# Attention scores in two fp32r passes, decay sums from two parts of g, later constants on GpSimd, and another planned order, in a one-core hybrid decoder layer

## The chip, the cores and the metric

The kernel runs on one core of a Trainium2 chip. The metric is the device time of one execution in microseconds (us).

## What is computed

One decoder layer on x of 256 tokens by 1024 channels, in float32: a normalisation, one combined input projection (1024 to 4104 columns), a softmax attention of 8 heads (64 wide, one key block of 256, so plainly causal, with ALiBi slopes), a gated delta rule of 4 heads (128 wide, chunks of 64), an output projection and a second normalisation, added to x. What the change touches, shortened:

```python
logit_own = einsum('hqd,hkd->hqk', qc, k_own) * scale - slopes[:, None, None] * dist_own
logit_own = where(dist_own >= 0, logit_own, NEG_INF)
p = softmax(logit_own, axis=-1)
...
gc = cumsum(g, axis=-1)
decay = exp(where(causal, gc[..., :, None] - gc[..., None, :], -inf))
a = where(strict, einsum('nbhid,nbhjd->nbhij', k_beta, k) * decay, 0.0)
t_inv = triangular_solve(a + eye, eye, lower=True, unit_diagonal=True)
...
r = xf * rsqrt(mean(xf * xf, axis=-1) + RMS_EPS)
```

## The kernel before

All calls are first recorded in a `Plan` and then put in order by a list scheduler (`Plan.run`, `Plan.order`), which has its own costs for every operation. It takes among the ready operations of an engine the one with the best rank, shifted by tables at lines 376 to 391: `MARGIN` (extra slack that the plan allows for results of TensorE, of the other engines and of loads), `BATCH` (a bonus for a matmul of the same row shape as the last), and `LEAD` (a bonus or malus for each stage). `emit` (line 354) then issues them, so in the profile nearly every instruction has line L372, and tiles tell them apart.

**Precision.** A float32 product is made from two parts of 12 bits (hi and lo, type fp32r) in three passes: hi by hi, hi by lo, lo by hi. ScalarE (ACT) copies the hi part, VectorE (DVE) subtracts it to get lo. TensorE (PE) runs fp32r products, and a few plain float32 ones.

**Stages.** The weights come in groups of 512 columns: dz (z and the b and a columns of the delta rule, in 8 pieces `raw_dz`), dk, dq, dv, then av, aq, ak, az for the attention, then the output weights. Each piece is loaded by SyncE's (SP) queue, split into hi and lo tiles (`dk_hi`, `dk_lo` and so on, five buffers of each), and multiplied with the transposed, normalised x (`hhi`, `hlo`). Forty-eight small matmuls on a zero tile (`ps_warm`) are put in by the plan where the engine would otherwise be thinly used.

**Head (lines 561 to 594).** For each of two halves t of the tokens: ACT squares one half of x, DVE the other, DVE adds the two sums and the epsilon (`rx<-ssq`), GpSimd (POOL) raises to the power -0.5 (`rx<-rx,pow`), ACT and DVE each scale half of x, PE transposes it (`hT`).

**GpSimd's constants (lines 470 to 540).** `blk`, `blks`, `lvl` (masks of the block inverse), `bias0` (printed as `bias`; causal mask and distances), `qscale`, and zeros in `yz` and in `qz` are written on POOL among the head's powers.

**Decay (lines 713 to 729).** `gneg` is minus log decay. For each t DVE makes `gs` (128x512, triu times gneg), and PE sums it with the strict lower triangle `strl` into `ps_d` in plain float32, then adds a mask in bf16. ACT takes its exponential (`dT`), which goes into the matrix whose inverse is built by stages `inv` and `dbl`: the recursion over `wc`, the spread to `wT`, two 32-square transposes (`xX`), products `ps_y` and `ps_w`, a second pair of transposes, products again. The state recurrence (`rec`) follows, then the output projection.

**Scores (lines 975 to 1016).** For each of 8 heads two parts, 128x128 and 128x256, each of three passes. Heads lie in pairs in 128 rows, 64 each; `qz` holds the scaled q with zeros in the other head's 64 rows, hi and lo apart; `ka_h` and `ka_l` hold the hi and lo parts of k for two pairs at a time.

**End (lines 1102 to 1126).** Each t has stores of 512 or 256 columns, all on SP's queue.

Of the kernel before, what the change touches and what calls it, by code (L numbers as in the profile page):

```python
# [123 lines left out]
class Plan:  # L124
# [24 lines left out]
    def record(self, eng, real, name, args, kw):  # L149
# [27 lines left out]
        if after:  # L177
            op.preds[self.ops[-1]] = True
# [202 lines left out]
BATCH = 0  # L381

MARGIN = [411, 175, 0]
# [6 lines left out]
LEAD = {"out0": 3258, "dk": 2097, "inv": -3594, "av": 2525, "dbl": -402, "out1": -1204, "att0": -470, "mixd": -508, "az": -1375}  # L390
# [4 lines left out]
def tile_hybrid(  # L395
# [22 lines left out]
    def const(shape, name, dtype=F32):  # L418
        return plan.tile(sb, shape, dtype, name)
# [4 lines left out]
    def sl(tag, shape, name, dtype=F32):  # L424
        return plan.tile(sb, shape, dtype, name, tag=tag)
# [57 lines left out]
    for t in range(NT):  # L483
        G.memset(yz16[:, of_chunk[t], :], 0.0)
# [4 lines left out]
    blk = const([P, NB, BASE], "blk")  # L489
    G.memset(blk, 1.0)  # L490
    G.affine_select(out=blk, in_=blk, pattern=[[-BASE, NB], [0, BASE]], compare_op=OP.is_ge,
                    fill=0.0, base=0, channel_multiplier=1)
    G.affine_select(out=blk, in_=blk, pattern=[[BASE, NB], [0, BASE]], compare_op=OP.is_ge,
                    fill=0.0, base=BASE - 1, channel_multiplier=-1)

    blks = const([P, NB, BASE], "blks")
    G.affine_select(out=blks, in_=blk, pattern=[[BASE, NB], [1, BASE]], compare_op=OP.is_gt,
                    fill=0.0, base=0, channel_multiplier=-1)

    strl = const([P, P], "strl")  # L500
# [5 lines left out]
    V.tensor_scalar(far16, strl, -NEG, None, op0=OP.mult)  # L506
# [3 lines left out]

    nl = P // (2 * BASE)
    lvl = const([P, nl, 2, BASE], "lvl")
    G.memset(lvl[:, :, 0, :], 0.0)
    G.memset(lvl[:, :, 1, :], 1.0)
    G.affine_select(out=lvl[:, :, 1, :], in_=lvl[:, :, 1, :], pattern=[[-2 * BASE, nl], [0, BASE]],
                    compare_op=OP.is_ge, fill=0.0, base=0, channel_multiplier=1)
    G.affine_select(out=lvl[:, :, 1, :], in_=lvl[:, :, 1, :], pattern=[[2 * BASE, nl], [0, BASE]],
                    compare_op=OP.is_ge, fill=0.0, base=BASE - 1, channel_multiplier=-1)


    bias0 = const([P, P + T], "bias0")
    G.iota(bias0[:, :P], pattern=[[1, P]], base=0, channel_multiplier=-1,
           allow_small_or_imprecise_dtypes=True)
    G.affine_select(out=bias0[:, :P], in_=bias0[:, :P], pattern=[[-1, P]], compare_op=OP.is_ge,
                    fill=NEG, base=0, channel_multiplier=1)
    G.iota(bias0[:, P:], pattern=[[1, T]], base=-P, channel_multiplier=-1,
           allow_small_or_imprecise_dtypes=True)
    G.affine_select(out=bias0[:, P:], in_=bias0[:, P:], pattern=[[-1, T]], compare_op=OP.is_ge,
                    fill=NEG, base=P, channel_multiplier=1)
    slopes = [2.0 ** -(h + 1) for h in range(HA)]  # L530

    qscale = const([P, HA // 2], "qscale")
    for h in range(HA):
        b = DA * (h % 2)
        G.memset(qscale[b : b + DA, h // 2 : h // 2 + 1], (DA ** -0.5) / slopes[h])

# [133 lines left out]

    vh = const([P, NT, HA * DA], "vh", F32R)
# [43 lines left out]
    gsa = sl("ms", HBB, "gs")  # L715
# [275 lines left out]
    for half in range(2):  # L991
        plan.stage = f"att{half}"
        ps = qps[half]
        for c in range(2):
            m = 2 * half + c
            for e in range(2):
                b = slice(DA * e, DA * e + DA)
                qs_ = qscale[b, m : m + 1]
                qh, ql = qz[m][b, 0, e, :], qz[m][b, 1, e, :]
                A.activation(qh, ps[b, c, :], AF.Copy, scale=qs_)  # L1000
                V.scalar_tensor_tensor(ql, ps[b, c, :], qs_, qh, op0=OP.mult, op1=OP.subtract)
        ps = kps[half]
        hm = slice(2 * half, 2 * half + 2)
        A.activation(kh[:, hm, :], ps, AF.Copy)
        V.tensor_tensor(kl[:, hm, :], ps, kh[:, hm, :], OP.subtract)
        for pr2 in range(2):
            m = 2 * half + pr2
            pTs = []
            for e in range(2):
                h = 2 * m + e  # L1010
                qh, ql = qz[m][:, 0, e, :], qz[m][:, 1, e, :]
# [96 lines left out]
    for t in range(NT):  # L1108
# [14 lines left out]
        for c0, cn in groups[t]:  # L1123
# [32 lines left out]
```

## Time and profile before

| | |
|---|---|
| runs (median of 3) | 174.79 us (174.78 to 174.94) |
| the profiled execution, its own time | 174.88 us |
| its span | 172.9 us |
| granted clock over the span | 0.989 |
| busy share | PE 95%, PEld 89%, DVE 78%, ACT 63%, POOL 12% |

The profiled execution is 0.09 us over the median, and 1.98 us of its time lie outside the span. Busy times are sums over instructions of the durations shown; matmuls overlap in the pipeline, so a matmul's own duration is longer than the distance from its start to the next one's start, and the distance is what it costs. The granted clock stands at 1.00 in every stretch of 10 us but the last.

### The profile page before, as it was taken

How to read it: one execution, taken by the hardware profiler on the slowest of the kernel's cores; microseconds unless marked ns; L12 is line 12 of the kernel's file. 1: busy time of each engine (PE TensorE's matmuls, PEld its weight loads, DVE VectorE, ACT ScalarE, POOL GpSimd, SP SyncE). 2: the span in 40 equal slices, each digit the busy share in tenths (PEclk: the TensorE clock that was granted, in tenths of full speed). 3: DMA queues.
4: the chain of work that ended last, by engine and by line, in shares of the span. 5: the costliest groups of instructions: out<-in, count | busy, mean ns of one | idle time of the engine just before them, and what ended most of it. 6: DMA issues, size and time to landing. Idle time of an engine off the chain costs nothing.

```text
span 172.9 us, 3465 instructions
## 1 busy us (share of the span) xinstructions
PE 164.1 (95%) x1311; PEld 154.1 (89%) x1311; DVE 134.7 (78%) x330; ACT 108.8 (63%) x231; POOL 21.2 (12%) x58
## 2 busy tenths in 40 slices
PE   7799999999999999999999999999999999999950
PEld 5589999997999999989999999999999998888850
DVE  4589566799579999898798999999689676474542
ACT  3689949968785545478554575665849594671230
POOL 8950000000000300400020000000001810000110
PEclk9999999999999999999999999999999999999995
DMA  5667689995776351067676108600000000640033
GB/s 193 232 224 261 224 271 241 391 317 136 207 233 161 91 189 57 5 205 276 222 245 200 69 0 251 238 0 0 8 0 4 2 0 0 196 172 0 3 118 121
DMA packets 12326, 24.92 MB, mean 144 GB/s; under 512 B 741, under 2 KB 1046, under 8 KB 12310
## 3 DMA queue, kind: packets, MB, share of 16 engines
q1 hardware_dynamic: 12310, 24.71, 44.1%
q8 instruction: 10, 0.16, 0.4%
q14 instruction: 6, 0.05, 0.1%
HBM read 23.65 MB, written 1.05 MB: 143 GB/s over the span
## 4 chain that ended last, share of the span: by engine, by line
PE 87%; POOL 5%; issue 4%; ACT 1%; DVE 1%; POOLq 0%; DVEq 0%
PE ps_out L372 10%; PE ps_av L372 9%; PE ps_az L372 7%; PE ps_dz L372 7%; PE ps_ak L372 7%; PE ps_dq L372 7%; PE ps_aq L372 7%; PE ps_dv L372 7%; PE ps_dk L372 7%; PE ps_s L372 3%; PE ps_y L372 2%; PE ps_w L372 2%; PE ps_gb L372 2%; PE ps_pt L372 2%; PE ps_d L372 1%
## 5 line engine op out<-in xcount | busy, mean ns | idle before, releaser
L372 DVE TENSOR_TENSOR o_lo<-raw_o,o_hi 128x1024 fp32r<-128x1024 f32 x8 | 9.8, 1220 | 5.1 <-ACT o_hi L372 5.1
L372 ACT ACTIVATE o_hi<-raw_o 128x1024 fp32r<-128x1024 f32 x8 | 8.4, 1056 | 5.0 <-PE ps_az L372 2.7
L372 ACT ACT_TABLE_LOAD x8 | 10.3, 1283 | 0.9 <-PEq L1143 0.8
L372 ACT ACTIVATE att_y<-att_y,mx 128x128 f32<-128x128 f32 (+1 forms) x16 | 7.2, 448 | 4.4 <-DVE mx L372 4.4
L372 PE MATMUL ps_az<-hlo,az_hi 128*128 128x256 f32 x32 | 9.8, 305 | 0.0
L372 PE MATMUL ps_az<-hhi,az_lo 128*128 128x256 f32 x32 | 9.6, 300 | 0.0
L372 PE MATMUL ps_aq<-hlo,aq_hi 128*128 128x256 f32 x32 | 9.6, 299 | 0.0
L372 PE MATMUL ps_az<-hhi,az_hi 128*128 128x256 f32 x32 | 9.5, 297 | 0.0
L372 PE MATMUL ps_warm<-wz 128*128 128x256 bf16 x48 | 8.3, 333 | 1.1 <-DVE wz L372 1.1
L372 PE MATMUL ps_aq<-hhi,aq_hi 128*128 128x256 f32 x32 | 9.3, 291 | 0.0
L372 PE MATMUL ps_aq<-hhi,aq_lo 128*128 128x256 f32 x32 | 9.2, 291 | 0.0
L372 PE MATMUL ps_dq<-hlo,dq_hi 128*128 128x256 f32 x32 | 9.1, 286 | 0.0
L372 PE MATMUL ps_dq<-hhi,dq_lo 128*128 128x256 f32 x32 | 9.1, 289 | 0.0
L372 PE MATMUL ps_ak<-hhi,ak_lo 128*128 128x256 f32 x32 | 9.1, 284 | 0.0
L372 PE MATMUL ps_ak<-hhi,ak_hi 128*128 128x256 f32 x32 | 9.1, 284 | 0.0
L372 PE MATMUL ps_dv<-hlo,dv_hi 128*128 128x256 f32 x32 | 9.1, 283 | 0.0
L372 PE MATMUL ps_dq<-hhi,dq_hi 128*128 128x256 f32 x32 | 9.0, 283 | 0.0
L372 PE MATMUL ps_dk<-hhi,dk_hi 128*128 128x256 f32 x32 | 9.0, 286 | 0.0
L372 PE MATMUL ps_dv<-hhi,dv_lo 128*128 128x256 f32 x32 | 9.0, 280 | 0.0
L372 PE MATMUL ps_ak<-hlo,ak_hi 128*128 128x256 f32 x32 | 9.0, 280 | 0.0
L372 PE MATMUL ps_dv<-hhi,dv_hi 128*128 128x256 f32 x32 | 9.0, 280 | 0.0
L372 PE MATMUL ps_dk<-hlo,dk_hi 128*128 128x256 f32 x32 | 8.9, 280 | 0.0
(254 smaller groups left out, 635.6 us busy)
## 6 DMA issues: line engine op xcount, KB each, us to landing
raw_o<-in_w_out_dram SPq DMA_DIRECT2D x4, 1024.0 KB, 5.0
raw_dz<-in_w_in_dram SPq DMA_DIRECT2D x8, 260.0 KB, 8.1
raw_dk<-in_w_in_dram SPq DMA_DIRECT2D x2, 1024.0 KB, 9.3
raw_dq<-in_w_in_dram SPq DMA_DIRECT2D x2, 1024.0 KB, 12.9
raw_dv<-in_w_in_dram SPq DMA_DIRECT2D x2, 1024.0 KB, 9.4
raw_av<-in_w_in_dram SPq DMA_DIRECT2D x2, 1024.0 KB
raw_aq<-in_w_in_dram SPq DMA_DIRECT2D x2, 1024.0 KB, 5.9
raw_ak<-in_w_in_dram SPq DMA_DIRECT2D x2, 1024.0 KB, 7.1
```

What stands on the lines that cost most here:

```text
L372: op.call(*args, **kw)
```

## The change

1. **Scores.** q of one head is put in the head's own 64 rows as the hi part and in the other 64 rows as the lo part; the hi part of k stands in both halves; the lo part of k stands in the head's own rows, with zeros in the other. One pass then gives hi by hi plus lo by hi, a second hi by lo. k is therefore split by (head, pair) in pieces of 64x256: 16 copies on ACT, 8 subtractions on DVE. The zeros are in `kl` instead of `qz`.
2. **Decay.** gneg is itself split (`gh`, `gl`), `gs` is made for both parts, and `strl` is fp32r, so that each t has two fp32r passes instead of one plain float32 product. The two parts lie in the slots `ms` and `wT`.
3. **GpSimd.** `blk`, `blks`, `lvl`, `bias0`, `qscale` and the zeros come behind a copy of `ba` (`held`), which DVE writes from the end of the first group (dz). The addition `rx<-ssq` moves from DVE to POOL; the epsilon goes into the reduction before it.
4. **Last store.** The second store of each t is issued by ACT's queue instead of SP's.
5. **Order.** New values of BATCH, MARGIN and LEAD.

```diff
@@ Plan.record
-            op.preds[self.ops[-1]] = True
+            op.preds[after if isinstance(after, Op) else self.ops[-1]] = True
@@ tables
-BATCH = 0
-MARGIN = [411, 175, 0]
+BATCH = 400
+MARGIN = [289, 0, 0]
-LEAD = {"out0": 3258, "dk": 2097, "inv": -3594, "av": 2525, "dbl": -402, "out1": -1204, "att0": -470, "mixd": -508, "az": -1375}
+LEAD = {"att0": 1788, "dbl": -699, "gates": 2282, "ak": 116, "out0": 206, "vt": 1330}
@@ constants
-    strl = const([P, P], "strl")
+    strl = const([P, P], "strl", F32R)
@@ head
-        V.tensor_tensor_reduce(junk[:, HD:], xs[t][:, HD:], xs[t][:, HD:], 1.0 / D, 0.0, op0=OP.mult, op1=OP.add,
+        V.tensor_tensor_reduce(junk[:, HD:], xs[t][:, HD:], xs[t][:, HD:], 1.0 / D, EPS, op0=OP.mult, op1=OP.add,
                                accum_out=ssq[:, t, 1:2])
         r = rx[:, t : t + 1]
-        V.tensor_scalar(r, ssq[:, t, 0:1], ssq[:, t, 1:2], EPS, op0=OP.add, op1=OP.add)
+        G.tensor_tensor(r, ssq[:, t, 0:1], ssq[:, t, 1:2], OP.add)
@@ after the group dz
+    G.tensor_copy(const([P, 2 * HG], "held"), ba[:, 0, :])
+    now = plan.ops[-1]
+    blk = const([P, NB, BASE], "blk")
+    G.memset(blk, 1.0, after=now)
...
+    for t in range(NT):
+        G.memset(yz16[:, of_chunk[t], :], 0.0, after=now)
@@ decay
-    gsa = sl("ms", HBB, "gs")
+    gpart = [const(GS, f"g{i}", F32R) for i in "hl"]
+    A.activation(gpart[0], gneg, AF.Copy)
+    V.tensor_tensor(gpart[1], gneg, gpart[0], OP.subtract)
+    gsa = [sl(g, HBB, f"gs{g}", F32R) for g in ("ms", "wT")]
...
-        gs = gsa[:, of_chunk[t], :]
-        V.tensor_tensor(gs, triu[:, None, :].to_broadcast(HB), gneg[:, t, :, None].to_broadcast(HB), OP.mult)
-        PE.matmul(pd, strl, gs, start=True, stop=False)
+        for i in range(2):
+            gs = gsa[i][:, of_chunk[t], :]
+            V.tensor_tensor(gs, triu[:, None, :].to_broadcast(HB), gpart[i][:, t, :, None].to_broadcast(HB), OP.mult)
+            PE.matmul(pd, strl, gs, start=i == 0, stop=False)
@@ scores
-    kh = const([P, HA // 2, T], "ka_h", F32R)
-    kl = const([P, HA // 2, T], "ka_l", F32R)
+    SET = [P, 2, 2, T]
+    q01 = const(SET, "qz", F32R)
+    k0, k1 = sl("s3", SET, "k0", F32R), sl("s2", SET, "k1", F32R)
+    qk2, kl2 = const(SET, "qk2", F32R), const([P, 2, T], "kl2", F32R)
+    sets = [(q01[:, 0], k0[:, 0], k0[:, 1]), (q01[:, 1], k1[:, 0], k1[:, 1]), (qk2[:, 0], qk2[:, 1], kl2)]
+    sets.append(sets[0])
...
-                A.activation(qh, ps[b, c, :], AF.Copy, scale=qs_)
-                V.scalar_tensor_tensor(ql, ps[b, c, :], qs_, qh, op0=OP.mult, op1=OP.subtract)
-        A.activation(kh[:, hm, :], ps, AF.Copy)
-        V.tensor_tensor(kl[:, hm, :], ps, kh[:, hm, :], OP.subtract)
+                A.activation(q[b, e, :], ps, AF.Copy, scale=qs_)
+                V.scalar_tensor_tensor(q[b2, e, :], ps, qs_, q[b, e, :], op0=OP.mult, op1=OP.subtract)
+                ps = kps[half][b, c, :]
+                A.activation(kh[b, e, :], ps, AF.Copy)
+                A.activation(kh[b2, e, :], ps, AF.Copy)
+                V.tensor_tensor(kl[b, e, :], ps, kh[b, e, :], OP.subtract)
...
-                    PE.matmul(o, qh[:, ts], kh[:, m, ks], start=True, stop=False)
-                    PE.matmul(o, qh[:, ts], kl[:, m, ks], start=False, stop=False)
-                    PE.matmul(o, ql[:, ts], kh[:, m, ks], start=False, stop=True)
+                    PE.matmul(o, q[:, ts], kh[:, ks], start=True, stop=False)
+                    PE.matmul(o, q[:, ts], kl[:, ks], start=False, stop=True)
@@ last stores
-            SP.dma_start(out[0, t * P : (t + 1) * P, cs], u[:, cs])
+            (AQ if i == 1 else SP).dma_start(out[0, t * P : (t + 1) * P, cs], u[:, cs])
```

How the order moves, at two places. First POOL in the head, before (names: `rx` the scale of x, `pow-1` the exponent, `bias`, `blks`, `lvl`, `qscale`, `yz` constants for later stages):

```order
L372 AFFINE_SELECT blks<-blk 128x128
L372 AFFINE_SELECT lvl<-lvl 128x4x16
L372 MEMSET qscale 64x1 x2
L372 MEMSET yz 128x512 x2
L372 TENSOR_TENSOR rx<-rx,pow-1_88 128x1
L372 IOTA bias_160 128x128
L372 IOTA bias_160 128x256
L372 AFFINE_SELECT bias_160<-bias_160 128x128
L372 AFFINE_SELECT bias_160<-bias_160 128x256
L372 TENSOR_TENSOR rx<-rx,pow-1_88 128x1
```

and the same engine and place now:

```order
L373 AFFINE_SELECT ident<-ident 128x128
L373 AFFINE_SELECT strl<-ones 128x128
L373 AFFINE_SELECT triu<-ones 128x128
L373 MEMSET pow_110 128x8
L373 TENSOR_TENSOR rx<-ssq 128x1
L373 TENSOR_TENSOR rx<-rx,pow-1_88 128x1
L373 TENSOR_TENSOR rx<-ssq 128x1
L373 TENSOR_TENSOR rx<-rx,pow-1_88 128x1
L373 COPY held<-ba 128x8
L373 MEMSET blk 128x128
```

The powers had constants ahead of them and between them; now the two additions and the two powers stand directly behind the four constants of the head, and the rest follows `held`.

Second DVE around the first pair of transposes of the block inverse (`xX`), before (`ka_l`, `qz` the lo parts of k and q, `az_lo` of a weight piece, `att_y` with `mx` the masked scores and their maximum):

```order
L372 STREAM_TRANSPOSE xX<-wT 128x512 x2
L372 TENSOR_TENSOR ka_l<-ps_ak_1265,ka_h 128x512
L372 TENSOR_TENSOR az_lo<-raw_az_1084,az_hi 128x1024
L372 SCALAR_TENSOR_TENSOR qz_1210<-ps_aq_1040,qscale,qz_1210 64x256
L372 TENSOR_TENSOR az_lo<-raw_az_1145,az_hi 128x1024
L372 ISA att_y_1429,mx<-ps_s_1371,bias_160 128x128
L372 ISA mx 128x1
```

and now (`k_386` is the set whose second part is the lo part of k):

```order
L373 STREAM_TRANSPOSE xX<-wT 128x512 x2
L373 TENSOR_TENSOR ak_lo<-raw_ak_1036,ak_hi 128x1024
L373 TENSOR_TENSOR az_lo<-raw_az_1172,az_hi 128x1024
L373 SCALAR_TENSOR_TENSOR qz<-ps_aq_1156,qscale,qz 64x256
L373 TENSOR_TENSOR k_386<-ps_ak_1189,k_386 64x256
L373 TENSOR_TENSOR az_lo<-raw_az_1172,az_hi 128x1024
L373 ISA att_y_1403,mx<-ps_s_1389,bias_392 128x128
L373 ISA mx 128x1
```

The first pair now comes ahead of two weight pieces `ak_lo` that stood ahead of it before, and until the second pair (of the same name) there are 15 rows before and 32 rows now: 2 `ak_lo`, 3 `az_lo`, 6 lo parts of q, 4 of k, maxima, reciprocals and four scalings of `att_y`, where before there were 1 `ka_l`, 3 `az_lo` and 3 lo parts of q beside the maxima. The multiplication `wT<-wT,ps_w`, which stands between the pairs, comes five rows ahead of the second pair before and two rows ahead now.

## Rows read from the trace of the kernel before

**Rows 1.** The page: busy times (part 1) and shares of the chain (part 4)

```profile
PE 164.1 (95%) x1311; PEld 154.1 (89%) x1311; DVE 134.7 (78%) x330; ACT 108.8 (63%) x231; POOL 21.2 (12%) x58
...
PE 87%; POOL 5%; issue 4%; ACT 1%; DVE 1%; POOLq 0%; DVEq 0%
```

**Rows 2.** Table by stretch: busy PE, PEld, DVE, ACT, POOL; clock, DMA, GB/s

```profile
100.00:120.00 20.00, 20.00 (x231) 19.22 (x230) 19.61 (x54) 12.93 (x31) 0.00 (x0) 1.00 0.31 106
120.00:140.00 20.00, 20.00 (x181) 20.00 (x180) 15.60 (x55) 13.80 (x47) 5.21 (x12) 1.00 0.01 3
```

**Rows 3.** Chain that ended last: start us, us, what

```profile
10.44 1.13 PE hT L372 x8
...
24.03 0.56 PE ps_warm L372 x5
...
25.39 9.16 PE ps_dk L372 x78
```

**Rows 4.** Timeline of POOL: start us, us, engine, line, operation, out<-in

```profile
5.52 0.99 POOL L372 MEMSET yz<- 128x512 f32 x2
6.47 0.57 POOL L372 TENSOR_TENSOR rx<-rx,pow-1_88 128x1 f32<-128x1 f32 x1
...
8.39 1.08 POOL L372 TENSOR_TENSOR rx<-rx,pow-1_88 128x1 f32<-128x1 f32 x1
```

**Rows 5.** Timeline of ACT in the head

```profile
6.20 0.19 ACT L372 ACTIVATION_READ_ACCUMULATOR xsq<-x 128x1 f32 x1
7.07 0.72 ACT L372 ACTIVATE x<-x,rx 128x512 f32<-128x512 f32 x1 [0.69 <-POOL rx L372]
...
9.51 0.72 ACT L372 ACTIVATE x<-x,rx 128x512 f32<-128x512 f32 x1 [0.55 <-POOL rx L372]
```

**Rows 6.** Timeline of DVE in the head

```profile
7.07 0.48 DVE L372 TENSOR_SCALAR x<-x,rx 128x512 f32<-128x512 f32 x1 [0.71 <-POOL rx L372]
...
8.35 0.70 DVE L372 TENSOR_TENSOR dz_lo<-raw_dz,dz_hi 128x520 fp32r<-128x520 f32 x1 [0.67 <-ACT dz_hi L372]
9.51 0.83 DVE L372 TENSOR_SCALAR x<-x,rx 128x512 f32<-128x512 f32 x1 [0.46 <-POOL rx L372]
```

**Rows 7.** Timeline of PE at the decay sums

```profile
40.52 1.02 PE L372 MATMUL ps_d<-gs,strl 128*128 128x512 f32 x2
41.38 0.38 PE L372 MATMUL ps_d<-far,ident 128*128 128x512 bf16 x1
```

**Rows 8.** Timeline of PE, fp32r matmuls of 512 columns in the output projection

```profile
162.46 0.39 PE L372 MATMUL ps_out<-o_hi,mixa_hi 128*128 128x512 f32 x1
162.69 0.40 PE L372 MATMUL ps_out<-o_lo,mixa_hi 128*128 128x512 f32 x1
```

**Rows 9.** Timeline of DVE, the products for the decay sums

```profile
37.49 1.28 DVE L372 TENSOR_TENSOR gs<-triu,gneg 128x512 f32<-128x512 f32 x2
```

**Rows 10.** Timeline of DVE in the attention stretch

```profile
100.27 1.30 DVE L372 STREAM_TRANSPOSE xX<-wT 128x512 f32<-128x512 f32 x2
101.60 0.69 DVE L372 TENSOR_TENSOR ka_l<-ps_ak,ka_h 128x512 fp32r<-128x512 f32 x1
102.21 1.22 DVE L372 TENSOR_TENSOR az_lo<-raw_az,az_hi 128x1024 fp32r<-128x1024 f32 x1
103.34 0.47 DVE L372 SCALAR_TENSOR_TENSOR qz<-ps_aq,qscale,qz 64x256 fp32r<-64x256 f32 x1
...
108.46 1.29 DVE L372 STREAM_TRANSPOSE xX<-wT 128x512 f32<-128x512 f32 x2
```

**Rows 11.** Timeline of ACT, the hi parts of q

```profile
90.02 1.92 ACT L372 ACTIVATE qz<-ps_aq,qscale 64x256 fp32r<-64x256 f32 x4
```

**Rows 12.** The page: group of ACT's table loads (part 5)

```profile
L372 ACT ACT_TABLE_LOAD x8 | 10.3, 1283 | 0.9 <-PEq L1143 0.8
```

**Rows 13.** Timeline of DVE and of SP's queue at the end

```profile
168.34 1.54 DVE L372 SCALAR_TENSOR_TENSOR u<-u,pr,x_again 128x512 f32<-128x512 f32 x3 [0.34 <-POOL pr L372]
169.12 1.30 SPq L372 DMA_DIRECT2D out_dram<-u  x3
```

More of the change, by code (lines that the diff above doesn't have):

```diff
@@ L481, in tile_hybrid @@
     G.memset(ones, 1.0)
-    for t in range(NT):
-        G.memset(yz16[:, of_chunk[t], :], 0.0)
     triu = const([P, P], "triu")
@@ L505, in tile_hybrid @@
     far16 = const([P, P], "far16", BF16)
-    V.tensor_scalar(far16, strl, -NEG, None, op0=OP.mult)
+    V.tensor_scalar(far16, strl.bitcast(F32), -NEG, None, op0=OP.mult)
     emod = const([P, BASE], "emod")
     V.tensor_reduce(emod, ident.rearrange("p (b k) -> p k b", k=BASE), op=OP.add, axis=AX.X)
[L511 to L535, printed above, removed]
     power = {}
@@ L668, in tile_hybrid @@
         A.activation(A_[t], z0[:, t, :], AF.Silu)
+    G.tensor_copy(const([P, 2 * HG], "held"), ba[:, 0, :])
+    now = plan.ops[-1]
+    blk = const([P, NB, BASE], "blk")
+    G.memset(blk, 1.0, after=now)
+    G.affine_select(out=blk, in_=blk, pattern=[[-BASE, NB], [0, BASE]], compare_op=OP.is_ge,
+                    fill=0.0, base=0, channel_multiplier=1, after=now)
+    G.affine_select(out=blk, in_=blk, pattern=[[BASE, NB], [0, BASE]], compare_op=OP.is_ge,
+                    fill=0.0, base=BASE - 1, channel_multiplier=-1, after=now)
+    blks = const([P, NB, BASE], "blks")
+    G.affine_select(out=blks, in_=blk, pattern=[[BASE, NB], [1, BASE]], compare_op=OP.is_gt,
+                    fill=0.0, base=0, channel_multiplier=-1, after=now)
+    nl = P // (2 * BASE)
+    lvl = const([P, nl, 2, BASE], "lvl")
+    G.memset(lvl[:, :, 0, :], 0.0, after=now)
+    G.memset(lvl[:, :, 1, :], 1.0, after=now)
+    G.affine_select(out=lvl[:, :, 1, :], in_=lvl[:, :, 1, :], pattern=[[-2 * BASE, nl], [0, BASE]],
+                    compare_op=OP.is_ge, fill=0.0, base=0, channel_multiplier=1, after=now)
+    G.affine_select(out=lvl[:, :, 1, :], in_=lvl[:, :, 1, :], pattern=[[2 * BASE, nl], [0, BASE]],
+                    compare_op=OP.is_ge, fill=0.0, base=BASE - 1, channel_multiplier=-1, after=now)
+    bias0 = const([P, P + T], "bias0")
+    G.iota(bias0[:, :P], pattern=[[1, P]], base=0, channel_multiplier=-1,
+           allow_small_or_imprecise_dtypes=True, after=now)
+    G.affine_select(out=bias0[:, :P], in_=bias0[:, :P], pattern=[[-1, P]], compare_op=OP.is_ge,
+                    fill=NEG, base=0, channel_multiplier=1, after=now)
+    G.iota(bias0[:, P:], pattern=[[1, T]], base=-P, channel_multiplier=-1,
+           allow_small_or_imprecise_dtypes=True, after=now)
+    G.affine_select(out=bias0[:, P:], in_=bias0[:, P:], pattern=[[-1, T]], compare_op=OP.is_ge,
+                    fill=NEG, base=P, channel_multiplier=1, after=now)
+    slopes = [2.0 ** -(h + 1) for h in range(HA)]
+    qscale = const([P, HA // 2], "qscale")
+    for h in range(HA):
+        b = DA * (h % 2)
+        G.memset(qscale[b : b + DA, h // 2 : h // 2 + 1], (DA ** -0.5) / slopes[h], after=now)
+    for t in range(NT):
+        G.memset(yz16[:, of_chunk[t], :], 0.0, after=now)
     vh = const([P, NT, HA * DA], "vh", F32R)
@@ L975, in tile_hybrid @@
     avT = sl("s4", [P, HA // 2, T], "avT")
-    qz = [plan.tile(sb, [P, 2, 2, T], F32R, f"qz{m}", tag=g) for m, g in enumerate(("qz", "s3", "s2"))]
-    qz.append(qz[0])
-    for q in qz[:3]:
+    SET = [P, 2, 2, T]
[4 more added lines that the diff above has]
+    sets.append(sets[0])
+    own = [slice(DA * e, DA * e + DA) for e in range(2)]
+    for _, _, kl in sets[:3]:
         for e in range(2):
-            G.memset(q[DA * (1 - e) : DA * (2 - e), :, e, :].bitcast(F32), 0.0)
-    kh = const([P, HA // 2, T], "ka_h", F32R)
-    kl = const([P, HA // 2, T], "ka_l", F32R)
+            G.memset(kl[own[1 - e], e, :].bitcast(F32), 0.0, after=now)
     mx = const([P, HA, 2], "mx")
@@ L992, in tile_hybrid @@
         plan.stage = f"att{half}"
-        ps = qps[half]
         for c in range(2):
             m = 2 * half + c
+            q, kh, kl = sets[m]
             for e in range(2):
-                b = slice(DA * e, DA * e + DA)
-                qs_ = qscale[b, m : m + 1]
-                qh, ql = qz[m][b, 0, e, :], qz[m][b, 1, e, :]
-                A.activation(qh, ps[b, c, :], AF.Copy, scale=qs_)
-                V.scalar_tensor_tensor(ql, ps[b, c, :], qs_, qh, op0=OP.mult, op1=OP.subtract)
-        ps = kps[half]
-        hm = slice(2 * half, 2 * half + 2)
-        A.activation(kh[:, hm, :], ps, AF.Copy)
-        V.tensor_tensor(kl[:, hm, :], ps, kh[:, hm, :], OP.subtract)
+                b, b2 = own[e], own[1 - e]
+                ps, qs_ = qps[half][b, c, :], qscale[b, m : m + 1]
+                A.activation(q[b, e, :], ps, AF.Copy, scale=qs_)
[4 more added lines that the diff above has]
+                V.tensor_tensor(kl[b, e, :], ps, kh[b, e, :], OP.subtract)
         for pr2 in range(2):
@@ L1010, in tile_hybrid @@
                 h = 2 * m + e
[L1011 removed]
+                q, kh, kl = (v[:, e, :] for v in sets[m])
                 ps_s = bank([P, P + T], f"ps_s{h}")
                 for o, ts, ks in ((ps_s[:, :P], slice(0, P), slice(0, P)), (ps_s[:, P:], slice(P, T), slice(0, T))):
[L1014 to L1016 removed]
+                    PE.matmul(o, q[:, ts], kh[:, ks], start=True, stop=False)
+                    PE.matmul(o, q[:, ts], kl[:, ks], start=False, stop=True)
                 y = tmp("att_p", [P, P + T], f"att_y{h}")
```

11 lines of the change are left out of this document (1 added, 10 removed).

## The prediction, made before the changed kernel was run

> **What bounds the kernel now.** I read the busy times first, then the chain of waits, then the stretches, then timelines of the places that the change touches. TensorE is busy 95% of the span and holds 87% of the chain that ended last [rows 1]. The reader should see that this is a full engine, not one that waits: from about 25 us on the chain is almost one string of matmuls, as the 78 of dk that take 9.16 us, 0.117 each [rows 3]. So a pass taken from TensorE is worth its whole pace, unless something else becomes late. Two places can be late. The head: the first two transposed halves of x come out of a string of GpSimd, ACT and PE pieces before the engine fills [rows 3 to 6]. And the attention stretch: from 100 to 120 us VectorE is busy 19.61 of 20 us, and only from 120 to 140 does it fall to 15.60 [rows 2]; there it is as full as TensorE, and the block inverse, whose transposes run on it [rows 10], feeds the state recurrence.
>
> The sum is made against the profiled execution's 174.88 us; the median of the runs is 0.09 less, which I take off at the end.
>
> **The change, part by part.**
>
> *Decay.* The plain float32 product of 512 columns holds TensorE from 40.52 to 41.38, 0.86 us [rows 7]. An fp32r pass of the same width goes on after 0.23 (162.46 to 162.69) [rows 8]. Each of two t trades 0.86 for two of 0.23: 2 x (0.86 - 0.46) = **-0.80 us**. VectorE gets two more products, 1.28 us together [rows 9], and ACT and VectorE one tiny operation each. They delay the first decay sum by about 1.5 us. TensorE has the dq group to run meanwhile, as it has around 40 us now, so I cost them at nothing; without that cover they are worth those 1.5 us. The Trainium skill, page "TensorE: Matmul & The Clock Gate", section "Back-to-back issue gap", gives a sustained 131 ns for a matmul of 512 columns: by that the decay would save about 1.2 us as an estimate. The rows show 0.23 for this kernel's type, and the measurement decides.
>
> *Scores.* Eight heads lose one pass of 128 and one of 256 columns. At 0.117 for 256 columns [rows 3], and half of that, 0.06, for 128: 8 x 0.177 = **-1.41 us** on TensorE. What pays: hi parts of k in 16 ACT copies of 64x256 (a quarter of 1.92 each, 0.48 [rows 11]: 7.7 us) in place of two of 128x512; lo parts in 8 subtractions of 64x256 (0.47 by the like one for q) in place of two of 0.69 [rows 10]: 8 x 0.47 - 1.38 = +2.4 us on VectorE. Each head's first score now waits for three small k pieces of its own pair instead of one large one.
>
> *Head.* POOL's first power starts at 6.47, behind zeros in yz until then; the second stands behind bias constants, and runs 8.39 to 9.47 [rows 4]. x is scaled at 7.07 and 9.51 right after [rows 5, 6]. In the new order the additions and powers are alone. The first scale is then bound by ACT's second square, which ends near 6.4 [rows 5]. The second sum is ready at the same time; with some 0.2 for the addition and 0.57 for the power [rows 4] its scale is there at 7.2, but ACT has the first scale and a dz_hi ahead of it, so about 8.05: 1.46 earlier than 9.51. The chain went through that scale, hT at 10.44 and the dz matmuls without a gap [rows 3], so dz ends 1.46 earlier. But the order now has 15 warm matmuls between dz and dk where it has 10; five cost 0.56 [rows 3]. Head: **-0.9 us**. Bounds: -1.3 if the second scale is not held by ACT, and +0.4 if the copies of dk come late, since ACT now has a table load (1.28 [rows 12]) and a copy of zt ahead of dk_hi, which eats the 0.9 and a little.
>
> *GpSimd's later constants.* They begin when ba is written, about 22 us, and the first is needed at the block inverse some 30 us later, the last near 100; POOL is busy 12% in all [rows 1]. Cost nothing; without the cover it would be the whole list, some 8 us of POOL beside the dk splits. What these pieces do to VectorE: the power beside dz_lo (two SBUF inputs) took 1.08 us instead of 0.57, while dz_lo took 0.70 for 520 columns, like the 0.69 of ka_l [rows 4, 6, 10]. So POOL is what is slowed. But the scale of x beside POOL zeros took 0.83 against 0.48 [rows 6], 0.35 lost. The Trainium skill, "GPSIMD Engine Reference", section "1. Specifications", says that GpSimd's SBUF interfaces are shared with VectorE and contend with VectorE instructions in a 2-port mode or with two SBUF inputs. It speaks against this part of the change; the first pair of rows shows the cost on POOL, the second some of it on VectorE, and it has a rival below.
>
> *ACT's table loads.* The order has 10 instead of 8: 2 x 1.28 us [rows 12], with 63% of ACT busy [rows 1]. Apart from the one ahead of dk_hi, bounded above, I cost them at nothing: they lie between decay exponentials, while TensorE runs dq and dv.
>
> *Last store.* The three issues of the second t take 1.30 us on SP from 169.12; the last product is done at 169.88 [rows 13]. With the middle one on ACT's queue the last issue starts at once instead of near 170.0: **-0.1** (0 to -0.2).
>
> *Order, and the wait that comes with it.* The first pair of transposes of the block inverse comes earlier: PE's part before it shrinks by 0.9 + 0.8, and two weight subtractions of 1.22 [rows 10] stand behind it now. But between the two pairs lay 6.9 us of VectorE work (101.57 to 108.46 [rows 10]), and by the rows of the order there are now about 12.8: the old ones, two more ak_lo (2.44), four k pieces for one large one (+1.2), three lo parts of q (1.4), and four scalings of attention rows. Behind wT's multiplication, which stands at the end of that, the second transposes and TensorE's second round of ps_y wait. By adding these durations I find the second pair near 111 to 112 instead of 109.8, with TensorE ready for it near 110.5: a wait of 0 to 2.2 us in place of what was hidden. TensorE has az and score matmuls to put in between, so I take **+0.7 us**.
>
> Sum: 174.88 - 0.80 - 1.41 - 0.90 - 0.10 + 0.70 = 172.37; less 0.09: **172.3 us**.
>
> **The rivals.**
>
> *No added wait* (az matmuls fill it all): 172.3 - 0.7 = 171.6. For it: TensorE has not idled in this stretch [rows 2]. Against: VectorE has 0.39 us of room there [rows 2].
>
> *The inverse and recurrence are the next bound.* Then what is saved in the scores turns into idle TensorE time while the recurrence goes its own way, and only what lies ahead of the chain counts: head 0.9, decay 0.8, store 0.1, so 174.88 - 1.8 - 0.09 = 173.0. For it: VectorE has 4.4 us free from 120 to 140 [rows 2], time in which it waits for chain steps.
>
> *The head gives nothing*: ACT's table load holds dk_hi; +0.4 instead of -0.9: 173.6. Against: dk_hi may come 1.3 us before TensorE asks.
>
> *GpSimd beside VectorE.* Five zeroings of 0.5 us or more, each taking 0.35 from VectorE [rows 6], delay dk's subtractions by up to 1.75: 174.05, say 174.0. Against: five buffers of each weight part, and the power's row.
>
> *The change does not do what it says*: the score matmuls wait for ACT's small copies as long as the dropped passes took (+1.41), and the head's gain is lost (+0.9): 172.3 + 2.3 = 174.6. For it: 16 copies, 7.7 us, in a stretch where ACT was busy 12.93 of 20 [rows 2].
>
> *Slower: VectorE sets the attention stretch.* Its net new work there is 2.4 (k pieces) and about 2.0 of the moved ak_lo, 4.4 us, in a stretch with 0.39 + 4.40 us free [rows 2]. If nothing is absorbed, TensorE waits 4.4 in place of my 0.7: 172.3 + 3.7 = 176.0. It decides against the kernel once the wait exceeds about 3.5 us, that is, when less than 0.9 of the 4.4 is absorbed. For it: the free time comes behind the second transposes, not before them. Against: much of TensorE's work in this stretch (ak, az) does not depend on those transposes.
>
> **How the numbers follow.** The forecast 0.37 (its own range, 171.9 to 172.9, comes from the bounds of wait and head); no added wait 0.19; recurrence 0.22; head gives nothing 0.05; GpSimd beside VectorE 0.03; no effect in scores and head 0.06; slower 0.08. A measurement tells about 0.2% (0.35 us) from no change. Faster by more than that takes in the first five: 0.86; within 0.2% (174.44 to 175.14): 0.06; slower 0.08. The range 171.0 to 174.0 holds the first four whole (0.83), from the no-wait case with a head gain of 1.3 up to the head-gives-nothing case with its wait somewhat larger.
>
> **What would show it.** Decay: two ps_d rows per t 0.23 apart, and none of 0.86. Scores: two ka passes per part, and 32 ps_s matmuls instead of 48. Head: the second scale of x near 8.05 on ACT, hT near 8.8, dz done by 22, dk's string from about 24.0 instead of 25.0. Wait: ps_y's second round near 110 to 112, and idle TensorE of less than a microsecond beside it. Wrong would be: gaps on TensorE between 100 and 140 of 2 us or more with VectorE as the releaser (the slower case, or the recurrence), a dk string that begins behind 25 us with ACT's dk_hi as the releaser, or k's small copies as the releaser of ps_s.

## The result, and the profile after

The changed kernel took 180.6 us (median of 4 runs, 179.29 to 182.1) against 174.87 for the kernel before: ratio 1.0303, 95% interval 1.0249 to 1.0357, so about 5.3 us slower. The forecast was 172.3, with a range up to 174.0. The ratios here and below leave out runs more than 1.5% above the fastest of the same kernel, here the one of 182.1. The profiled execution, the fastest of the four, took 179.29 with a span of 177.6. The others have no profile; their mean granted clocks, 0.958, 0.958 and 0.944 against its 0.967, show that the clock was down in them too, for longer.

The page's busy times, its row of the granted clock in 40 slices of 4.4 us, and the chain's shares, to be read against [rows 1]:

```profile
PE 167.5 (94%) x1295; PEld 156.7 (88%) x1295; DVE 138.9 (78%) x337; ACT 114.7 (65%) x248; POOL 21.1 (12%) x61
...
PEclk9999999999999999999999999985599999999998
...
PE 78%; ACT 9%; issue 5%; DMA 3%; DVE 1%; SPq 1%; POOLq 0%; POOL 0%; DVEq 0%; ACTq 0%
```

TensorE has 16 matmuls less and yet is busy 3.4 us longer; the clock row falls in the 27th slice and to a half in the 28th and 29th; ACT holds 9% of the chain instead of 1%. The head first, in the chain that ended last (start, us, what), against [rows 3]:

```profile
8.79 1.16 PE hT L373 x8
9.95 11.57 PE ps_dz L373 x96
22.02 1.74 PE ps_warm L373 x15
23.76 11.31 PE ps_dk L373 x96
```

This is what was forecast, and a little more: hT at 8.79 (8.8 said), dk's string from 23.76 (24.0 said). The second scale of x starts on ACT at 8.03 (8.05 said), and each decay sum has two fp32r passes and none of 0.86. Up to 90 us the changed kernel is ahead. Then the stretches: window, busy us (instructions) of PE, PEld, DVE, ACT, POOL; then clock, DMA share, GB/s; against [rows 2]:

```profile
90.00:100.00 10.00, 10.00 (x86) 9.96 (x85) 5.55 (x8) 5.58 (x9) 0.00 (x0) 1.00 0.01 2
100.00:110.00 10.00, 9.40 (x77) 8.88 (x76) 9.19 (x26) 9.15 (x23) 0.00 (x0) 1.00 0.81 276
110.00:120.00 10.00, 8.31 (x105) 7.14 (x104) 8.71 (x30) 8.56 (x24) 0.00 (x0) 0.91 0.11 41
120.00:130.00 10.00, 10.00 (x68) 9.65 (x67) 6.05 (x18) 4.35 (x13) 0.00 (x0) 0.58 0.01 2
```

Three things follow each other here. From 90 to 100 VectorE and ScalarE are half idle. From 100 to 120 both are nearly full (ACT 17.71 of 20 us against 12.93 before, DVE 17.90, which is less than its 19.61 before) and TensorE stands still for 0.60 + 1.69 = 2.29 us. Then its clock is down, which by these rows costs 10 x 0.09 + 10 x 0.42 = 5.1 us. That is an estimate which takes TensorE to be the bound all the while. In pieces of 2 us:

```profile
112.00:114.00 2.00, 1.69 (x33) 1.36 (x31) 1.93 (x10) 1.94 (x6) 0.00 (x0) 1.00 0.03 8
114.00:116.00 2.00, 0.66 (x9) 0.57 (x9) 1.36 (x4) 1.94 (x8) 0.00 (x0) 1.00 0.00 0
116.00:118.00 2.00, 2.00 (x39) 1.74 (x37) 1.69 (x6) 1.92 (x7) 0.00 (x0) 1.00 0.00 0
118.00:120.00 2.00, 2.00 (x15) 1.73 (x13) 1.75 (x6) 0.84 (x3) 0.00 (x0) 0.56 0.00 0
126.00:128.00 2.00, 2.00 (x11) 2.00 (x11) 1.77 (x8) 1.62 (x6) 0.00 (x0) 0.50 0.00 0
128.00:130.00 2.00, 2.00 (x17) 2.00 (x17) 0.67 (x2) 2.00 (x7) 0.00 (x0) 0.88 0.01 4
```

The clock goes to 1.2 GHz just after 118, some 3 us behind the end of the long stop, and is back at 2.4 just after 128. TensorE's timeline shows a short stop for the lo part of k, the long stop and the lower pace (az matmuls of 256 columns 0.21 us apart, not 0.117):

```profile
108.55 0.47 PE L373 MATMUL ps_s<-k,qz 128*128 128x128 f32 x2 [0.34 <-DVE k L373]
...
112.82 0.90 PE L373 MATMUL ps_y<-xX,bT 32*32 32x32 f32 x26
115.34 0.37 PE L373 MATMUL ps_y<-xX,bT 32*32 32x32 f32 x6 [1.61 <-ACT yz L373]
...
126.64 0.41 PE L373 MATMUL ps_az<-hhi,az_hi 128*128 128x256 f32 x1
126.85 0.41 PE L373 MATMUL ps_az<-hlo,az_hi 128*128 128x256 f32 x1
```

And ScalarE's timeline shows what stood ahead of that yz, although ps_y's first results were there at 113:

```profile
110.59 1.06 ACT L373 ACTIVATE o_hi<-raw_o 128x1024 fp32r<-128x1024 f32 x1
111.67 0.38 ACT L373 ACTIVATE qk<-ps_ak 64x256 fp32r<-64x256 f32 x1
111.95 0.47 ACT L373 ACTIVATE att_pTh<-ps_pt 128x384 fp32r<-128x384 f32 x1
112.45 0.77 ACT L373 ACTIVATE qk<-ps_ak 64x256 fp32r<-64x256 f32 x2
113.23 0.49 ACT L373 ACTIVATE att_pTh<-ps_pt 128x384 fp32r<-128x384 f32 x1
113.73 0.38 ACT L373 ACTIVATE qk<-ps_ak 64x256 fp32r<-64x256 f32 x1
114.12 0.38 ACT L373 ACTIVATE k<-ps_ak 64x256 fp32r<-64x256 f32 x1
114.41 0.39 ACT L373 ACTIVATE att_y<-att_y,mx 128x128 f32<-128x128 f32 x1
...
114.91 0.37 ACT L373 ACTIVATE yz<-ps_y 32x256 f32<-32x256 f32 x1
```

Five small k pieces (at 111.67, 112.45 twice, 113.73 and 114.12) stand ahead of yz. In the kernel before one copy of all of that k stood in their place, and yz followed the exponential behind it at 111.39:

```profile
110.19 0.60 ACT L372 ACTIVATE ka_h<-ps_ak 128x512 fp32r<-128x512 f32 x1 [1.22 <-PE ps_ak L372]
...
111.39 0.38 ACT L372 ACTIVATE yz<-ps_y 32x256 f32<-32x256 f32 x1
```

### The profile page after: what moved, and what is told of

It is laid out like the page before. It is cut to its first block, busy times and chain, and to the rows that moved or that the text cites. A ratio compares the mean times of both kernels' runs of the same rounds, so it can differ in the third digit from the quotient of the medians.

```text
span 177.6 us, 3450 instructions
## 1 busy us (share of the span) xinstructions
PE 167.5 (94%) x1295; PEld 156.7 (88%) x1295; DVE 138.9 (78%) x337; ACT 114.7 (65%) x248; POOL 21.1 (12%) x61
## 4 chain that ended last, share of the span: by engine, by line
PE 78%; ACT 9%; issue 5%; DMA 3%; DVE 1%; SPq 1%; POOLq 0%; POOL 0%; DVEq 0%; ACTq 0%
PE ps_out L373 10%; PE ps_av L373 9%; PE ps_dz L373 7%; PE ps_dq L373 6%; PE ps_dv L373 6%; PE ps_dk L373 6%; PE ps_az L373 6%; PE ps_ak L373 5%; PE ps_aq L373 5%; DMA raw_dz<-in_w_in_dram 3%; PE ps_gb L373 2%; PE ps_s L373 2%; PE ps_w L373 2%; ACT k L373 2%; ACT qz L373 2%
## 5 line engine op out<-in xcount | busy, mean ns | idle before, releaser
L373 PE MATMUL ps_dv<-hhi,dv_lo 128*128 128x256 f32 x32 | 9.5, 296 | 0.0
L373 PE MATMUL ps_aq<-hlo,aq_hi 128*128 128x256 f32 x32 | 9.0, 280 | 0.0
L373 PE MATMUL ps_dz<-dz_hi,hlo 128*128 128x264 f32 (+1 forms) x32 | 8.9, 284 | 0.0
```

The source lines that it names most:

```text
L373: op.call(*args, **kw)
```

## The experiments

Four theories were set against each other at first. **A**: a stop of TensorE is what lets the clock fall. **B**: the clock falls because the scores now have fewer matmuls, stop or not. **K** and **O**: the stops come from the small k pieces (K), or from the new tables of the order (O). In the experiments that keep an order, a hook behind the planner moves named instructions and leaves the rest where they stood. Times are medians with the range of the runs; the median of before was 174.8 to 174.9 beside each of them. Where it is said that the clock held or fell in an execution without a profile, its mean granted clock tells it.

**Is the clock lost through the stop?** Two kernels fill the stop at 113.5, one with work that is due anyway, one with work of no use.

```diff
+    part = [op for op in pe[at:] if tag_of(op) == "ps_az0"][:16]   # at: the 14th ps_y32
+    pe[at:at] = part
```

> The changed kernel with one edit of the order: the next 16 az matmuls (their data are there since 106.4) stand inside the second round of ps_y, where TensorE stood still from 113.5 to 115.3. Theory A (the stop makes the clock fall to 1.2 GHz from 118 to 128): the stop is filled, 1.8 us, and the clock stays, 5.0 us: 179.3 - 6.8 = 172.5. Theory B (the clock falls because this stretch has fewer and smaller matmuls since the scores lost a pass, stop or not): only the stop is filled, 177.5, and the clock still falls.

```diff
+                if count == 13:                                     # behind the 13th ps_y32
+                    for _ in range(15):
+                        op.call(b.full[:, 256:512], h[:, 0, :P], h[:, 0, :], start=True, stop=True)
```

> The changed kernel with 15 matmuls more, of no use, at the same place (256 columns each, into the free half of the bank of ps_y): no useful work comes earlier, so this prices the clock alone. Theory A: the clock stays at 1.00, 179.3 - 5.0 = 174.3. Theory B: the clock falls all the same, 179.3.

Measured: 176.1 (175.65 to 179.4) and 175.8 (175.64 to 180.12). The clock held in five of seven and five of six executions (mean 0.99 or more, and 0.97 or less in the other three), where it fell in all four of the changed kernel. Of the useless matmuls an execution at 180.12 was profiled, with the clock down again, while five others took 175.6 to 176.0:

```profile
110.00:120.00 10.00, 9.38 (x115) 8.32 (x114) 8.00 (x28) 8.15 (x22) 0.00 (x0) 0.96 0.09 33
120.00:130.00 10.00, 10.00 (x66) 9.42 (x65) 6.20 (x19) 3.99 (x10) 0.00 (x0) 0.53 0.01 2
```

So the same instructions take 4.3 us more or less with the clock down or up. The two rows give 10 x 0.04 + 10 x 0.47 = 5.1 us for this fall, as they do for the changed kernel's, so this estimate is some 0.8 us too high. And the fall is not a certain one: a little more or less work in that stretch decides. This speaks for A. But work in the stop did not pay (176.1, not 172.5; and 175.8, not 174.3): in the filled kernel TensorE stood still elsewhere, 0.41 us at 120 to 130 and 0.83 at 140 to 150, which is a third of what is missing there:

```profile
120.00:130.00 10.00, 9.59 (x93) 8.80 (x90) 8.45 (x25) 5.18 (x15) 0.00 (x0) 1.00 0.01 2
...
140.00:150.00 10.00, 9.17 (x64) 7.96 (x62) 7.78 (x14) 6.98 (x14) 1.76 (x2) 1.00 0.42 156
```

**Tables or parts?**

```diff
-BATCH = 400 / MARGIN = [289, 0, 0] / LEAD of the change
+BATCH = 0 / MARGIN = [411, 175, 0] / LEAD of before
```

> All of the change but its tables: BATCH, MARGIN and LEAD of before. Theory O (the new tables place the q and k evictions late and ScalarE's queue then holds the inverse): 172 to 173, no stop between 100 and 120 of over 1 us, clock 1.00. Theory K (the 12 added ScalarE copies alone make ScalarE late in that stretch, in any order): slower than before, a stop behind ScalarE's k copies, clock low for some us, 176 or more.

and the same three tables the other way round, in the kernel before:

> The kernel before with the new BATCH, MARGIN and LEAD and nothing else. Theory O: the stretch is starved here too, 177 or more. Theory K: within 1 us of before, 174 to 176, no fall of the clock.

Measured: 175.7 (173.45 to 177.56, 10 runs; clock 0.66 from 110 to 120 in the profiled one, of 176.05) and 176.8 (176.51 to 177.45; ratio 1.0126, interval 1.0092 to 1.0160). Neither theory by itself: the tables alone cost 1.9 us at a clock of 1.00, with only 0.8 us of stops from 100 to 120, so that an order can also cost time in which no stop is shown. The parts alone let the clock fall in six of ten executions, though in the four where it held (173.45 to 174.36) they beat before. What the tables do is seen in the kernel before with them, from 90 to 100:

```profile
90.00:100.00 10.00, 10.00 (x87) 10.00 (x87) 5.31 (x6) 4.53 (x6) 0.00 (x0) 1.00 0.11 40
```

VectorE is as idle there as in the changed kernel (5.55); with the old order it was busy 8.89. aq and ak run side by side, so their first halves come out 7 us later or more (first q piece on ACT at 98.93 here and at 97.59 in the changed kernel, before at 90.02 [rows 11]), and all their evictions fall behind 97.

**Which part?** Scores alone, with the old tables (diff: the score hunks of the change); and the change without them:

> The kernel before with the two-pass scores and nothing else (old tables, so planned anew). The sum gives -1.4 us, 173.5, if nothing waits. Theory K (the small k copies make ScalarE's queue late between 100 and 120 us, TensorE stops, and the clock falls in some executions): TensorE loses 1 us or more in 100 to 120 against 0 before, the clock falls in some executions; 174 to 178. Theory O (the tables are what hurts): 173.5, clock 1.00.

> The change without its scores and without its tables: three-pass scores, old BATCH, MARGIN and LEAD; decay in two parts, GpSimd's later constants, the additions on GpSimd, the last store. My terms for these: -0.8 - 0.9 - 0.1 = -1.8, 173.1. Theory K: 173.1 with no fall of the clock, better than before and than the change with the old tables. If the clock falls here too, the scores are not its cause, and 175 or more.

Measured: 177.2 (175.34 to 181.59) and 173.87 (173.82 to 173.94; ratio 0.9951, interval 0.9934 to 0.9968). The scores alone bring stops (1.22 us from 110 to 120) and the fall, in three executions of four; the rest is faster than before, with the clock up in all four. In the scores kernel yz is late on ACT's queue as well: its first input was there near 112, and it stands behind seven pieces of k. But TensorE had az matmuls to run meanwhile, and its own stops there name VectorE. ScalarE's rows first, then TensorE's:

```profile
109.85 1.06 ACT L372 ACTIVATE o_hi<-raw_o 128x1024 fp32r<-128x1024 f32 x1
110.92 1.16 ACT L372 ACTIVATE qk<-ps_ak 64x256 fp32r<-64x256 f32 x3
112.10 1.58 ACT L372 ACTIVATE k<-ps_ak 64x256 fp32r<-64x256 f32 x4
113.71 0.37 ACT L372 ACTIVATE yz<-ps_y 32x256 f32<-32x256 f32 x1
...
111.19 1.15 PE L372 MATMUL ps_y<-xX,bT 32*32 32x32 f32 x28 [0.64 <-DVE xX L372]
113.30 0.55 PE L372 MATMUL ps_pt<-ident,att_y 128*128 128x128 f32 x3 [0.48 <-DVE dT L372]
```

**Fewer matmuls, or the pieces?** The kernel before in its own order, without the hi by lo pass (that product is missing from its scores):

```diff
+            if op.eng == "pe" and tag_of(op)[:4] == "ps_s" and not kw["start"] and not kw["stop"]:
+                continue
```

> The kernel before in its own order, with the middle pass (hi by lo) of the scores left out and nothing else: 16 matmuls less, 1.41 us by the paces of before; q and k are split as before. Theory B (the clock falls because the scores have fewer matmuls): the clock falls between 105 and 125 in some executions, 175 to 179. Theory K (the small pieces of k are at fault, not the missing passes): the clock holds in all, 173.4 to 174.5.

Measured: 173.84 (173.76 to 173.89; ratio 0.9942, interval 0.9925 to 0.9959), clock up in all four. B falls for this order: the missing pass alone does not bring the clock down. And of its 1.41 us only 1.0 arrive; TensorE now waits at the products of VectorE's second transposes:

```profile
110.00 1.09 PE L426 MATMUL ps_y<-xX,bT 32*32 32x32 f32 x32 [0.76 <-DVE mx L426]
```

**Take yz's wait away in the scores kernel.** Its order, with two instructions of ACT ahead, and the 16 ps_y matmuls of TensorE, which stood apart, put together:

```diff
+    i = next(i for i, op in enumerate(act) if op.stage == "att1" and tag_of(op) == "k0")
+    act[i:i] = [both yz32]
+    pe[at:at] = ys                     # ys: the 16 ps_y32, taken from their places
```

> The kernel before with the two-pass scores alone, in the order of that run, but on ScalarE the two copies yz of the second round of the inverse stand ahead of the last four copies of k instead of behind them (1.6 us earlier), and the 16 ps_y matmuls stand together. Theory K: TensorE's stops between 110 and 114 shrink by up to 1 us (the wait for the second transposes, 0.8, stays), the clock falls later or not: 174.5 to 176. If ScalarE's queue is not it: 175.3 to 181 as without the edit.

Measured: 174.67 (174.57 to 176.74; nine of ten under 174.8), against 177.2. With both yz at 112.41 and right behind, and not at 113.71 and 115.00, it takes 2.6 us less and the clock holds in nine of ten, and this with TensorE still standing 1.56 us between 110 and 120:

```profile
110.00:120.00 10.00, 8.44 (x124) 7.39 (x122) 9.75 (x33) 7.55 (x22) 0.00 (x0) 1.00 0.34 107
```

That is nearly as much as in the changed kernel, and more than the 1.22 us of the scores kernel without the edit, so a sum of stops does not tell whether the clock falls. Nor do the two stops shown above: they are still there, 0.65 and 0.36 us for 0.64 and 0.48. By what the edit holds the clock is not shown. The like in the changed kernel:

> The changed kernel in its own order, but on ScalarE the two copies yz stand ahead of two copies of k and a softmax exponential (by 1.2 us), and the 16 ps_y matmuls stand together, so that the last three don't wait for the first yz. Theory K: the stop of 1.8 us at 113.5 shrinks to about 0.6, the clock holds in some executions: 175 to 178, where it holds about 175. If the stop was not ScalarE's: 179 to 182.

Measured: 180.5 (179.98 to 181.29), a miss. The stop only moved, and grew:

```profile
118.12 1.03 PE L436 MATMUL ps_w<-wT,yz 32*32 32x32 f32 x16 [2.37 <-DVE wT L436]
```

VectorE's order has the reciprocal of a softmax sum ahead of wT's subtraction, and that now waited 1.72 us for ScalarE's exponential, which both yz had passed:

```profile
116.86 0.17 DVE L436 RECIPROCAL rs<-sm 128x2 f32<-128x2 f32 x1 [1.72 <-ACT att_y L436]
```

wT followed at 117.57 and TensorE at 118.12. Here both queues are late, not one instruction.

**Copies off ScalarE.** The second copy of each k piece made by GpSimd from the first (`G.tensor_copy(kh[b2], kh[b])`), planned anew with the old tables, and in the unchanged order of the changed kernel:

> All of the change with the old tables, and the second copy of each hi part of k made by GpSimd from the first one, instead of by ScalarE from PSUM (8 of 64x256). Theory K: ScalarE loses 8 x 0.38 = 3.0 us in that stretch, the clock falls in fewer executions or none, 172.5 to 174. If ScalarE's copies are not what holds TensorE: as with the old tables, 173.5 to 176, some executions with the clock down.

> The changed kernel in its own order, every instruction where it stood, except that the eight second copies of k leave ScalarE's queue and are made by GpSimd from the first ones. Theory K (ScalarE's queue is what ps_y waits for from 113.5 to 115.3): the stop shrinks by the two or three copies that stood ahead of it, about 1 us, to under 1 us, the clock may hold, 175 to 177. If ScalarE's copies are not it: the stop of 1.8 us remains, 179 to 182.

Measured: 177.6 (175.41 to 181.04) and 178.7 (174.31 to 179.45). In the kept order TensorE stood still 0.86 us from 110 to 120 instead of 1.69, so ScalarE's copies were about half of that stop, and one execution took 174.31; in the other three the clock fell all the same. Planned anew, it was slower than with ScalarE's copies (175.7), outside both expectations; its long stops, 0.86 and 1.09 us, wait for VectorE. Taking 3 us from ScalarE is not enough. Whether that is because VectorE is nearly as full, or because GpSimd's copies are slow themselves (0.40 to 0.93 us each in the kept order), was not tried apart.

**A better order for the parts.** The change with the old tables, wT, the second transposes and the first softmax scaling earlier on VectorE:

```diff
+    new = [0, 2, 4, 5, 7, 8, 1, 3, 6, 9, 11, 14, 12, 15, 16, 10, 13, 17, ...]
+    q[a : a + 27] = [q[a + k] for k in new]                        # q: VectorE's queue
```

> All of the change with the old tables, in the order of that run, but on VectorE wT's subtraction and the second transposes stand ahead of two lo parts of k and one of q, and the first softmax scaling ahead of a weight piece. Two stops of TensorE stood there, 0.74 us for the transposes and 0.60 for the scaling, and the clock fell right behind them in most executions. If these stops are what lets the clock fall: both shrink to under 0.3, the clock holds, 172.3 to 173.5 in all executions, better than both kernels. If not (theory B): 173 to 176 with the clock falling in most.

Measured: 173.77 (173.42, 173.62, 173.93 and one of 178.87; ratio 0.9930, interval 0.9914 to 0.9947). It is the fastest version with all the parts (its tables are the old ones), and beats both kernels, but in one execution of four the clock still fell: the stop for the transposes went, and a wait of 1.02 for a lo part of k took its place.

**What in the tables?** Four more kernels: the new tables without the scores, the old MARGIN alone, and the planner's price of ScalarE's small copies corrected (`+ 125 * (rows == 64)`), with either tables.

> The whole change with its new tables, but with the three-pass scores of before. The new tables alone cost 1.9 us, the other parts alone give 0.9 to 1.8. If the stops need both the late evictions of the new tables and the small k pieces: 174.5 to 176, the clock holds. If the new tables alone let the clock fall: 177 or more.

> The changed kernel with MARGIN of before (411, 175, 0) and the new BATCH and LEAD. If the smaller margins are what makes the plan too tight for the small pieces: the stops of 2.3 us before 116 shrink, the clock falls seldom, 173.5 to 176. If it is BATCH and LEAD, which run aq and ak side by side and so bring the evictions of q 7 us later: 177 to 181.

> The changed kernel, planned with 125 ns more for each ScalarE operation of 64 rows: four copies of 64x256 in a row take 0.39 us each in the trace, while the plan counts 0.26. If the plan's belief in ScalarE is the cause: the order places yz and wT ahead of late k pieces, 173 to 176, the clock falls seldom. If not: 178 or more.

> All of the change with the old tables, planned with the same 125 ns more. Without it 173.5 to 176 with the clock down in most executions. If the plan's price of the small copies matters: 172.5 to 174, the clock holds. If not, as without it.

Measured: 176.57 (176.18 to 182.22, two of five with the clock down); 173.98 (173.82 to 174.37, seven runs; ratio 0.9961, interval 0.9945 to 0.9976); 177.2 (173.53 to 179.85); 175.8 (175.55 to 179.21). So the new tables with the other parts let the clock fall even without the scores, and the changed kernel with one line put back, MARGIN, is faster than before. The corrected price gave executions of 173.5 and others of 180 with the new tables, and a fall in all four with the old: it doesn't settle it. In the kernel with the old MARGIN the evictions start earlier, and VectorE is busy from 90 to 100:

```profile
90.00:100.00 10.00, 10.00 (x88) 9.97 (x86) 8.65 (x18) 8.11 (x16) 0.00 (x0) 1.00 0.33 107
100.00:110.00 10.00, 9.50 (x101) 8.98 (x100) 9.63 (x30) 7.07 (x18) 0.00 (x0) 1.00 0.33 105
```

Is it slack as such?

> The changed kernel with only the first margin (slack for results of TensorE) put back to 411, the second (for the other engines' results) left at 0. With both put back it took 174.0, clock up in all seven. If the margin for TensorE's results is what matters: 174 to 175, clock up. If the one for ScalarE's and VectorE's results, whose lateness stops TensorE: 176 to 181, clock down in some executions.

> The changed kernel with margins larger than before's: 600 and 350. If slack in the plan is the cause, more of it also keeps TensorE from stopping: 173 to 175, clock up in all. If 174.0 with the old margins was the luck of one order: anything from 173 to 181, with the clock falling in some.

Measured: 178.7 (175.06 to 180.68) and 176.8 (175.21 to 177.65; ratio 1.0110, interval 1.0052 to 1.0168). The first entry alone does not help, so the second matters beside it; but more of both is worse again, with the clock down in three of four. So MARGIN decides through the order that it happens to give, and a larger one is no cure. Which feature of an order makes the clock fall stays open. In all, the clock fell with the scores alone, and with the tables and the other parts without the scores, but with neither the tables alone nor the other parts alone (four executions each).

## Why the prediction was wrong

**Head: right, mis-sized by a half.** The fourth dk matmul starts at 25.34 before and at 23.96 after, 1.38 us earlier, where 0.9 was said; ACT's table load ahead of dk_hi (priced as a bound) cost nothing. **Decay:** as said in kind. **Last store:** issued as said, but it gave next to nothing: from the last product to the end of the span it is 3.02 us, against 3.06 before. The change without scores and tables gives 0.9 to 1.0 us of the 1.8 summed; most of the rest is lost behind 100 us without a stop that the profile names, and is left open. **GpSimd's constants:** nothing on dk_lo. The four dk_lo beside them took 1.216 us on the mean, against 1.220 before, and it is the GpSimd side that stretched, up to 1.37 for one selection. But small operations of VectorE were longer there: `bet` took 0.58 us beside the zeros of yz, where it took 0.17 before, 0.41 more, so the 0.35 that the prediction took for one zeroing has its like.

```profile
25.91 0.17 DVE L372 TENSOR_SCALAR bet<-bet 128x8 f32<-128x8 f32 x1
...
24.86 0.58 DVE L373 TENSOR_SCALAR bet<-bet 128x8 f32<-128x8 f32 x1
...
24.88 1.03 POOL L373 MEMSET yz<- 128x512 f32 x2
```

The first row is of the kernel before, the others of the changed one. It did not reach TensorE, whose string of dk matmuls runs on, so the rival that summed 1.75 us of it did not come.

**Scores: the gain exists, but not whole.** Without the pieces the dropped pass gives 1.0 of 1.41. That the score matmuls would wait for k's small pieces, named as a sign of being wrong, came in small: 0.16 and 0.34 us, with VectorE's lo part as the releaser.

**The step that failed is the wait, with what hung on it.** I took +0.7 us, bounded by 0 and 2.2, for TensorE waiting for the second transposes on VectorE. The transposes came when they were said to, from 110.92 to 112.43, and az matmuls filled TensorE until then. The stops were 2.29 us in all, just above the upper bound, and the long one, 1.61, stood behind them and waited for ScalarE's yz:

```profile
110.92 0.70 DVE L373 STREAM_TRANSPOSE xX<-wT 128x512 f32<-128x512 f32 x1
...
111.73 0.70 DVE L373 STREAM_TRANSPOSE xX<-wT 128x512 f32<-128x512 f32 x1
```

So the size of the bound was nearly right by luck, and the queue was the wrong one. I had priced ScalarE's 16 copies (7.7 us) and put nothing of it in the sum, without a reason; they stood only in a rival, as a wait of the scores. But the new order moved the evictions behind 97 us, so that they met the exponentials and the inverse's copies, and ACT was busy 17.71 of 20 us. The rows of the order that I showed for this stretch were VectorE's alone. The rival *slower* named VectorE, with 176.0 from 4.4 us more work on it; but VectorE was less busy from 100 to 120 than before (17.90 for 19.61), and what was late was ScalarE's queue: first its yz, and with yz put ahead (180.5) VectorE's wT, itself behind ScalarE's exponential.

**The larger part had no term at all.** The granted clock stood at 1.00 before, up to 160 us (0.95 from 160 to 170, where TensorE's work ends), and I took every pace at that level. The fall to 1.2 GHz cost 4.3 us by the executions with the useless matmuls, 5.1 by the rows. Together: 174.88 - 0.80 - 1.41 - 1.38 + 2.29 + 4.3 = 177.9, or 178.7 with 5.1, against 179.29 measured; 0.6 to 1.4 us is not accounted for.

The rival *the recurrence is next* is not seen at work: TensorE is full from 130 to 150 in both kernels.

## What to carry to other kernels

A pass taken from a full engine is paid for on the engines that prepare its operands: count their small pieces in the stretch where they fall, on each queue that a serial chain passes through, and look at the new order of all of these queues, not of the one that was full before. Where TensorE's work is thinned beside a serial chain, a fall of its clock belongs among the rivals with a price (here 4 to 5 us, more than all gains together), and times must be taken in many executions, since the same instructions ran at either level here. When an order is searched for with a plan's numbers, vary the parts and the tables apart: here the parts with one line of the old tables were 0.8 us faster than before, and with the new line 5.3 slower.

## What the runs showed of the hardware that was not expected

The clock held with 1.56 us of stops between 110 and 120 in one kernel (the scores alone with yz ahead), and fell behind 1.69 us in another and 1.22 in a third (the scores alone). Within one kernel it held or fell from execution to execution, 4.3 us apart.

A small TENSOR_SCALAR of VectorE took 0.58 us beside GpSimd's zeroing and 0.17 in the kernel before, while the subtractions of 1024 columns took no longer beside GpSimd's selections (1.216 for 1.220).

ScalarE's copies of 64 rows follow each other more slowly than those of 128 rows, at the same 256 columns. The changed kernel's timeline of ScalarE, with both types of output:

```profile
28.29 0.65 ACT L373 ACTIVATE zt<-ps_dz 128x256 f32<-128x256 f32 x2
...
117.35 1.16 ACT L373 ACTIVATE k<-ps_ak 64x256 fp32r<-64x256 f32 x3
126.73 0.75 ACT L373 ACTIVATE avT<-ps_av 64x256 f32<-64x256 f32 x2
```

With 0.38 us for one, the next starts 0.27 later in the first row and 0.37 to 0.39 later in the others. So a copy of half the rows took no less of the queue here than a whole one, but more: splitting k by rows cost more than its elements say. That it is the number of rows, and not where in the tiles they lie, was not tried by itself.
